# Moving the second conv chunk's taps, the staging slots and the first banks of the down product in a decoder layer's kernel

## The chip, the core and the metric

The kernel runs on one core of one Trainium2 chip. The metric is the device time of one execution in microseconds; several executions are timed and their median is given. One further execution is recorded by the hardware profiler, and all rows of a trace come from that one.

## What is computed

One layer of a hybrid decoder on 1024 tokens and 16 meta tokens put in front of them (T = 1040 rows of 1024 channels), all in float32:

```
h = LN(concat(meta, x))
z = h @ w_in + b_in   ->  q | k | v | c_val, c_gate | g_attn, g_conv
a = attention(q, k, v)          # window 128, 8 heads, 2 key heads, a sink each, 16 meta keys for all
c = silu(LN(dwconv31(c_val * sigmoid(c_gate))))
mixed = sigmoid(g_attn) * (a @ w_attn_proj) + sigmoid(g_conv) * (c @ w_conv_proj)
h = LN(alpha * h + mixed @ w_out)
u, g = dwconv3(h @ ffn_w_up)
out = LN(alpha * h + (gelu(g) * u) @ ffn_w_down)   # the 16 meta rows are dropped
```

The depthwise convolution over 31 taps has 512 channels: four chunks of 128 channels, one per partition.

## The kernel before

**Order of the work.** The program is written once, in a sequence, and a scheduler then fixes the order on each engine and each DMA queue when the kernel is built. It plays the program through with its own cost of every instruction; of those that are due by then, the one with the lowest number in `cur_priority` (or in a `rank` around it) goes next. `after(a, b)` puts a behind b in that order and adds no wait. On the chip each engine runs its own list strictly in that order, and SP's list holds most DMA issues, so an instruction that waits holds up everything behind it in its list. Waits come from data alone: a write waits for earlier readers and writers of the same columns of a tile. The tile FA (128 x 6144 float32) is used by many steps one after the other, and its column ranges count, not its names.

**Precision.** TensorE multiplies in a reduced float32 form, so every operand is split in two: a high half by a ScalarE copy and a low half by a VectorE subtraction (L303 to L307 for weights). Each product takes three matmuls (`product`, L338): lines 342, 345 and 346.

**The z stage (L349 on).** The product h @ w_in is made in tiles of 128 output channels; each takes 8 x 3 matmuls for each of four column groups (`z_group`). There are three PSUM banks for the groups (`ps_z`, tag "mm", bufs=3), and each is emptied by its own `evac`. The first three tiles (k, v, q of the first head pair) are written out by hand in three groups of 272, 384 and 384 columns (L482 to L646). The residual products (L293, L294), 18 of them on VectorE, keep the normalized input times alpha for later.

**Staging slots.** `stage(n)` (L368) gives a place in FA where ScalarE puts an evicted group before it goes on: k on its way to DRAM (L377), q before its split (L393, L395, L396), a gate's sigmoid (L695, L696), a merge gate's tanh (L724). Before, there are five slots, 400 columns apart, from column 4104.

**Conv chunks (L689).** A chunk makes its gate tile (`g_evac`, tanh by ScalarE), then its value tile, whose groups VectorE multiplies with the sigmoid into `cin` (`v_evac2`, L703). `cin` has two buffers, taken in turn: chunk 1, chunk 0, chunk 2, chunk 3. Then 31 taps follow on VectorE, one instruction each over 1026 columns (L713 the first, L715 the other thirty), into `acc[c]`, at a rank behind everything else (60000 and 100 more for each chunk). The coefficients `cdw` are loaded at L671. Chunks 1 and 0 come before attention; chunks 2 and 3 come between the merge gates (`order`, L930), which are the work that fills TensorE while attention waits.

**Values and keys.** `vT` = FA[:, 0:1040] holds v transposed. It is turned back by transposes on TensorE (L766, L774) and split (L769, L778, L779). k comes back from DRAM into FA from column 2054 (`kr`, L748) and is copied to `Kx` (L755, L757). `vd` is a broadcast of the bias table to all partitions in DRAM, from which the bias tiles are read (L730 on).

**Attention.** For each block and each head one bank `ps_s` is filled (L887, L888) and emptied by VectorE (L891), and then come exponentials, transposes (L911) and the product with v (L922 to L924).

**Up and down products.** The up product (L1526) uses four tiles of two PSUM banks each, in this order: pw, px, pz, py. The last one to be written in each pass is py, and VectorE empties it (L1534). The result f goes to DRAM (`f_out`, L1462). The down product has eight accumulators of one bank each: `X` and `Z`, four each (L1583). Its operands come in pairs (f and weights) from `operand` (L1603): a load into a raw place, then the two split instructions (L1613, L1614). Six pairs are made ahead.

```
F_RAW = [RXF[:, 0:1024], RXF[:, 1024:2048]] + [FA[:, i * 1024:(i + 1) * 1024] for i in range(6)]
W_RAW = [None, None] + [OB[:, i * 1024:(i + 1) * 1024] for i in (2, 3, 0, 1)]
```

`None` is one of two weight buffers. Columns 0 to 4096 of FA also hold the temporaries of the up product's convolution (`ftmp`), eight of 512 columns in turn.

Of the kernel before, what the change touches and what calls it, by code (L numbers as in the profile page):

```python
# [29 lines left out]
P = 128  # L30
# [82 lines left out]
def tile_hybrid_layer(  # L113
# [6 lines left out]
    def dram(ap, offset, dims):  # L120
        return bass.AP(tensor=ap.tensor, offset=ap.offset + offset, ap=[list(d) for d in dims])

    def load(o, i):
        return nc.sync.dma_start(out=o, in_=i)
# [156 lines left out]
    def h0(k, hl, a, b):  # L281
        return (RHO, RHC)[hl][:, k * T + a:k * T + b]
# [34 lines left out]
        return [t[:, o:o + D] for o in W_FLAT]  # L317

    fills, cin_done, gate_mm, gate_last = [0], [], {}, []
    last_fill, last_split = [], []  # L320

    def weights(shape, fill):
        fills[0] += 1
# [14 lines left out]
    def product(ps, terms, behind=None):  # L338

        n = len(terms)  # L340
        for i, (ah, al, bh, bl) in enumerate(terms):
            ins = nc.tensor.matmul(ps, al, bh, start=i == 0, stop=False)  # L342
            if i == 0 and behind is not None:
                after(ins, behind)
            nc.tensor.matmul(ps, ah, bh, start=False, stop=False)  # L345
            last = nc.tensor.matmul(ps, ah, bl, start=False, stop=i == n - 1)  # L346
        return last

    def z_group(wt, g, a, b, evac):  # L349
        hi, lo = wt  # L350
        ps = pat.tile([P, 512], F, name="ps_z", tag="mm", bufs=3)
        last = product(ps[:, :b - a], [(hi[:, k], lo[:, k], h0(k, 0, a, b), h0(k, 1, a, b)) for k in range(KC)])
        with rank(RK_EVAC):
            evac(g, a, b, ps[:, :b - a])
        return last
# [9 lines left out]

    st_next = [0]

    def stage(n, lo=4104, cnt=5):  # L368
        i = st_next[0] % cnt
        st_next[0] += 1  # L370
        return FA[:, lo + i * 400:lo + i * 400 + n]

    tc.cur_priority = RK_QKV + 1000

# [293 lines left out]
    att = ExitStack()  # L668
    cp = att.enter_context(tc.tile_pool(name="cin", bufs=2, side="right", reuse_waits="tile"))
    cdw = cp.tile([P, TAPS * CH], F, name="cdw", tag="cdw", bufs=1)  # L670
    load(cdw, cols_in[:, n_kept:])  # L671
    ap = att.enter_context(tc.tile_pool(name="att", bufs=1, side="right", reuse_waits="tile"))

    Kx = [ap.tile([P, NB, 144], R, name=f"kx{g}") for g in range(NKV)]
# [9 lines left out]
    tc.cur_priority = RK_QKV + 1000  # L684


    acc = [FA[:, c * U:(c + 1) * U] for c in range(CH)]

    def conv_chunk(c):  # L689
        sig = {}  # L690
# [36 lines left out]
        gate_mm[i] = z_tile(in_cols(14 + i), TG, gate_evac)  # L727

    tc.cur_priority = RK_QKV + 2000
    after(load(vd, dram(v1d, 0, [[0, P], [J_LEN, NH], [1, J_LEN]])), last_fill[-1])  # L730
    load(bias[:, :, 0:P], dram(vd, 127, [[L8 - 1, P], [J_LEN, NH], [1, P]]))
    load(bias[:, :, 144:272], dram(vd, 127 + P, [[L8 - 1, P], [J_LEN, NH], [1, P]]))
    load(bias[:, :, P:144], dram(vd, J_META, [[L8, P], [J_LEN, NH], [1, 16]]))
# [1 line left out]
    load(biasq, dram(vd, J_METAQ + 1, [[L8 - 1, 2], [J_LEN, NH], [1, 16]]))  # L735

    tc.cur_priority = RK_QKV + 4000
    taps = [conv_chunk(1)]
    cin4 = cin_done[-1]
    vmT = ap.tile([P, 64], F, name="vmT")  # L740
    after(nc.vector.memset(vmT, 0.0), cin4)
    for hl in range(2):
        for g in range(NKV):
            vm_ins = nc.vector.tensor_copy(vmT[g * HD:(g + 1) * HD, hl * 32 + g * 16:hl * 32 + g * 16 + 16],
                                  vT[g * HD:(g + 1) * HD, 0:16])
    tc.cur_priority = RK_QKV + 1000
    for g in range(NKV):
        kr = FA[:, 2054 + g * T:2054 + (g + 1) * T]  # L748
        for h in range(2):
            load(kr[h * HD:(h + 1) * HD, :T], kd[g * HD:(g + 1) * HD, :])  # L750
        for lo in (0, 64):
            for o, i in ((Kx[g][lo:, :, 16:144], kr[lo:, 16:T].rearrange("p (n c) -> p n c", c=P)),
                         (Kx[g][lo:, :, 0:16], kr[lo:, 0:16].unsqueeze(1).to_broadcast([P - lo, NB, 16]))):
                if lo == 0:
                    ins = nc.vector.tensor_copy(o, i)  # L755
                else:
                    ins = nc.vector.tensor_tensor(o, i, f32(o), OP.subtract)  # L757
                after(ins, vm_ins)
    ones = ones_of(cp, vm_ins)
    for t in [vm] + pmTs:  # L760
        after(nc.vector.memset(f32(t[64:]), 0.0), vm_ins)
    tc.cur_priority = RK_QKV + 4000
    taps.append(conv_chunk(0))
    tc.cur_priority = RK_QKV + 2000
    ps = pat.tile([P, 512], F, name="ps_vm", tag="t", bufs=2)
    after(nc.tensor.transpose(ps[:64, :P], vmT, ident), gate_last[-1][2])  # L766
    src = ps[:64, :P].rearrange("p (g d) -> p g d", d=HD)
    nc.scalar.copy(vm[:64, :, 0], src)
    nc.vector.tensor_tensor(vm[:64, :, 1], src, f32(vm[:64, :, 0]), OP.subtract)  # L769
    for q4 in range(2):  # L770
        ps = pat.tile([P, 512], F, name="ps_v4", tag="t", bufs=2)
        for i in range(4):
            c = NMETA + (q4 * 4 + i) * P
            after(nc.tensor.transpose(ps[:, i * P:(i + 1) * P], vT[:, c:c + P], ident), gate_last[-1][2])  # L774
        src = ps[:, :].rearrange("p (n g d) -> p n g d", g=2, d=HD)
        for g in range(NKV):
            hi, lo = (V[:, q4 * 4:q4 * 4 + 4, g, i] for i in range(2))
            nc.scalar.copy(hi, src[:, :, g, :])  # L778
            nc.vector.tensor_tensor(lo, src[:, :, g, :], f32(hi), OP.subtract)  # L779
    for t in taps:  # L780
        t()
    tc.cur_priority = RK_QKV + 5000
    for r in range(1, 4):
        z_tile(in_cols(r), TG, q_evac(r))


# [793 lines left out]
    oa_stack.close()  # L1580
    dn = ctx.enter_context(tc.tile_pool(name="dn", bufs=1, side="left", reuse_waits="tile"))
    pdn = ctx.enter_context(tc.tile_pool(name="pdn", bufs=1, space=PSUM, reuse_waits="tile"))
    X, Z = ([pdn.tile([P, 512], F, name=f"ps_{n}", tag=f"d{j}") for j in b]  # L1583
            for n, b in (("x", (0, 1, 6, 7)), ("z", (2, 3, 4, 5))))


    def blk(t, first, step, col):
# [8 lines left out]
    W_DN = [(OC, OC_UP + i * 2048) for i in range(4)] + [(RHC, 4096 + R_DN), (RHC, 6144 + R_DN), (RHO, 6144 + R_DN)]  # L1596
    F_RAW = [RXF[:, 0:1024], RXF[:, 1024:2048]] + [FA[:, i * 1024:(i + 1) * 1024] for i in range(6)]
    W_RAW = [None, None] + [OB[:, i * 1024:(i + 1) * 1024] for i in (2, 3, 0, 1)]
    PAIRS = [(j, min(2, FH - j)) for j in range(0, FH, 2)]

    los, evacs = [], []

    def operand(i, src, j, n, raws, places):  # L1603
        raw = raws[i % len(raws)]
        if raw is None:
            raw = wraw([P, D])
        raw = raw[:, :n * 512]
# [5 lines left out]
        nc.scalar.copy(hi, raw)  # L1613
        los.append(nc.vector.tensor_tensor(lo, raw, f32(hi), OP.subtract))  # L1614
        if len(los) > 1:
            after(los[-1], evacs.pop() if evacs else los[-2])
        return hi, lo
# [187 lines left out]
```

## Time and profile before

| | |
|---|---|
| three timed executions | 1282.48, 1283.21, 1283.51 us; median 1283.21 |
| the profiled execution | 1284.34 us, span 1282.6 us from first to last instruction |
| mean granted clock of TensorE | 0.992 |
| instructions | 23049 |
| DMA | 212.19 MB, 165 GB/s on average |

How to read the rows: times are microseconds from the start of the span. A row of the timeline has start, duration, engine (PE = TensorE, PEld its weight loads, DVE = VectorE, ACT = ScalarE, SPq and ACTq the DMA issues of SyncE and ScalarE), line, operation, what is written <- what is read, shapes, count, and in brackets the engine's idle time before it and what ended that. In the slices of the page, each digit is a fortieth of the span, in tenths. A row of waits has the total, the number of times and the longest. A row of a stretch has its length, the busy time of PE, PEld, DVE, ACT and POOL with counts, the granted clock, the DMA share and GB/s.

### The profile page before, as it was taken

Reading aid. Unit: us, or ns where it says so; the run is one execution under the profiler, and the core shown is the slowest. Engines: PE = TensorE matmul, PEld = TensorE weight load, DVE = VectorE, ACT = ScalarE, POOL = GpSimd, SP = SyncE. Lnnn points to the kernel's source line nnn. Section 1 sums busy time; section 2 is a strip of 40 time slices with the busy share of each in tenths; the row PEclk is TensorE's granted clock in tenths of the full one; section 3 lists DMA queues with packets and bytes.
Section 4 is the critical chain, followed back from the end, with each engine's and each line's share of the span. In section 5 each row is a group of like instructions: output and inputs, shape, how many; then the busy total and the mean of one; then the engine's idle time right before and its main releaser. Section 6 shows DMA issues by size and latency. Waiting matters only on the chain.

```text
span 1282.6 us, 23049 instructions
## 1 busy us (share of the span) xinstructions
PE 1260.1 (98%) x9194; PEld 1187.8 (93%) x9194; DVE 1076.1 (84%) x1862; ACT 586.0 (46%) x1080; POOL 18.6 (1%) x16
## 2 busy tenths in 40 slices
PE   7999998999999999999999999999999999999997
PEld 7899998999999999788899999999999997888886
DVE  7879999999969466547899999999899986888697
ACT  5423344555455232344654554555555553535330
POOL 2200000001000000000000000000000000000000
PEclk8999998999999999999999999999999999999999
DMA  6275742432445565222235455453455556989722
GB/s 247 82 243 144 185 116 73 120 89 76 111 117 146 158 170 141 91 83 83 83 105 206 174 208 177 186 211 123 164 189 191 193 204 240 394 289 389 264 75 82
DMA packets 98701, 212.19 MB, mean 165 GB/s; under 512 B 11411, under 2 KB 38611, under 8 KB 98338
## 3 DMA queue, kind: packets, MB, share of 16 engines
q1 hardware_dynamic: 84474, 199.64, 46.7%
q10 hardware_dynamic: 14120, 11.08, 2.8%
q8 instruction: 72, 1.18, 0.4%
q14 instruction: 35, 0.29, 0.1%
HBM read 150.29 MB, written 62.70 MB: 166 GB/s over the span
## 4 chain that ended last, share of the span: by engine, by line
PE 92%; DVE 5%; DMA 1%; issue 1%; ACT 1%; SPq 0%; POOL 0%; DVEq 0%; ACTq 0%
PE px L1526 14%; PE py L1526 9%; PE ps_x L1651 9%; PE ps_z L342 8%; PE ps_z L346 8%; PE ps_z L345 8%; PE ps_z L1651 5%; PE pz L1526 5%; PE pw L1526 5%; PE ps_p L346 2%; PE ps_p L342 2%; PE ps_p L345 2%; PE ps_w L346 2%; PE ps_w L342 2%; PE ps_w L345 2%; PE ps_z L548 1%
## 5 line engine op out<-in xcount | busy, mean ns | idle before, releaser
L346 PE MATMUL ps_z<-RHC,w 128*128 128x256 f32 (+2 forms) x864 | 244.5, 283 | 0.0
L342 PE MATMUL ps_z<-RHO,w 128*128 128x256 f32 (+2 forms) x864 | 244.5, 283 | 0.0
L345 PE MATMUL ps_z<-RHO,w 128*128 128x256 f32 (+2 forms) x864 | 243.8, 282 | 0.0
L342 PEld LDWEIGHTS ps_z<-RHO,w 128*128 128x128 f32 x864 | 163.2, 189 | 0.9 <-issue 0.3
L346 PEld LDWEIGHTS ps_z<-RHC,w 128*128 128x128 f32 x864 | 163.4, 189 | 0.6
L345 PEld LDWEIGHTS ps_z<-RHO,w 128*128 128x128 f32 x864 | 163.3, 189 | 0.4
L715 DVE SCALAR_TENSOR_TENSOR FA<-cin,cdw,FA 128x1026 f32<-128x1026 f32 x120 | 152.3, 1278 | 0.2
L1348 DVE TENSOR_TENSOR RHO<-wr,RHO 128x512 fp32r<-128x512 f32 x94 | 63.8, 687 | 7.9 <-ACT RHO L1347 7.8
L1347 ACT CAST RHO<-wr 128x512 fp32r<-128x512 f32 x94 | 56.7, 619 | 25.7 <-DVE wr L1365 11.6
L307 DVE TENSOR_TENSOR w<-wr,w 128x1024 fp32r<-128x1024 f32 x37 | 45.1, 1219 | 26.8 <-ACT w L304 26.7
L304 ACT CAST w<-wr 128x1024 fp32r<-128x1024 f32 x37 | 38.8, 1047 | 54.7 <-PE ps_z L346 36.4
L1365 DVE TENSOR_TENSOR wr<-wr 128x512 f32<-128x512 f32 x88 | 60.4, 686 | 0.1
L724 ACT ACTIVATE FA<-ps_z,colr 128x258 f32<-128x258 f32 (+1 forms) x64 | 30.1, 471 | 58.9 <-PE ps_z L346 48.3
L1538 ACT COPY FA<-px 128x514 f32<-128x514 f32 (+2 forms) x23 | 13.1, 571 | 76.5 <-PE px L1526 76.5
L1348 DVE TENSOR_TENSOR w<-wr,w 128x512 fp32r<-128x512 f32 x60 | 40.7, 688 | 4.9 <-ACT w L1347 4.7
L1526 PE MATMUL px<-OA,RHO 128*128 128x258 f32 x324 | 43.2, 282 | 0.0
L1453 ACT ACTIVATE FA<-OB,coll 128x512 f32<-128x512 f32 x44 | 35.9, 815 | 14.6 <-DVE OB L1534 14.6
L1347 ACT CAST w<-wr 128x512 fp32r<-128x512 f32 x60 | 36.3, 618 | 12.8 <-DVE wr L1365 6.4
L1526 PE MATMUL px<-RHC,RHO 128*128 128x258 f32 (+1 forms) x312 | 41.1, 281 | 0.8 <-ACT OB L1538 0.8
L1526 PE MATMUL px<-OC,RHO 128*128 128x256 f32 x324 | 41.5, 277 | 0.0
L1538 ACT COPY OB<-px 128x514 f32<-128x514 f32 (+2 forms) x46 | 26.1, 567 | 32.1 <-PE px L1526 31.9
L1526 PEld LDWEIGHTS px<-OA,RHO 128*128 128x128 f32 x324 | 40.5, 189 | 0.2 <-ACT OB L1538 0.2
(441 smaller groups left out, 3314.2 us busy)
## 6 DMA issues: line engine op xcount, KB each, us to landing
wr<-in_w_up_dram SPq DMA_DIRECT2D x44, 512.0 KB, 3.6
wr<-in_w_z_dram SPq DMA_DIRECT2D x29, 512.0 KB, 3.9
fd<-FA SPq DMA_DIRECT2D x44, 256.0 KB, 2.1
OB<-in_w_down_dram SPq DMA_DIRECT2D x21, 512.0 KB, 3.7
FA<-sd SPq DMA_DIRECT2D x15, 512.0 KB, 9.1
qt<-qd SPq DMA_DIRECT2D x28, 256.0 KB, 4.1
sgd<-FA ACTq DMA_DIRECT2D x48, 128.0 KB, 2.4
td<-OB SPq DMA_DIRECT2D x12, 512.0 KB, 2.6
```

The source lines that it names most:

```text
L304: ins = nc.scalar.copy(hi, raw)
L307: return nc.vector.tensor_tensor(lo, raw, f32(hi), OP.subtract)
L342: ins = nc.tensor.matmul(ps, al, bh, start=i == 0, stop=False)
L345: nc.tensor.matmul(ps, ah, bh, start=False, stop=False)
L346: last = nc.tensor.matmul(ps, ah, bl, start=False, stop=i == n - 1)
L715: nc.vector.scalar_tensor_tensor(acc[c], cin[:, j:j + U], wc, acc[c], OP.mult, OP.add)
L1347: nc.scalar.copy(hi, src)
L1348: ins = nc.vector.tensor_tensor(lo, src, f32(hi), OP.subtract)
L1365: ins = nc.vector.tensor_tensor(*x)
L1526: ins = nc.tensor.matmul(o, x[:, ks], bmat(sub, q, hl, k), start=first and k + j == 0, stop=k == 3 and j == 2, skip_group_check=not first)
L1538: copied.append(nc.scalar.copy(*x))
L1651: nc.tensor.matmul(banks[i], l[:, ts], r[:, ws], start=first and a and x + k == 0, stop=z and x == len(ops) - 1 and k == 2, skip_group_che ...
```

## The change

It has seven parts.

1. `z_group` puts the first matmul of each group behind the last of the group before it in the program, for all groups that it makes.
2. `stage` has seven slots, 280 columns apart, from column 4146, in place of five, 400 apart, from 4104.
3. `acc` lies at columns 0, 1040, 2066 and 3092 in place of 0, 1026, 2052 and 3078, so that acc[1] no longer shares columns with `vT`; `kr` moves to 2066 and ends where the slots begin.
4. The load of `vd` is put behind the load of `cdw`.
5. Chunk 1's taps are called right behind its input; chunk 0's taps stay behind the V transposes. K copies, memsets and the meta values come behind chunk 0's input rather than chunk 1's.
6. q tile 1 comes ahead of the V transposes, which were behind the third group of chunk 0's gate.
7. The down product's accumulators are allocated in the order of their numbers; X is 0, 1, 6, 7 as before and Z is 4, 5, 2, 3. The first six operand pairs use raw places 0, 1, 2, 3, 0, 1, and the later ones go on from place 4.

```diff
-        last = product(ps[:, :b - a], [(hi[:, k], lo[:, k], h0(k, 0, a, b), h0(k, 1, a, b)) for k in range(KC)])
+        last = product(ps[:, :b - a], [(hi[:, k], lo[:, k], h0(k, 0, a, b), h0(k, 1, a, b)) for k in range(KC)],
+                       z_last[-1] if z_last else None)
+        z_last.append(last)
...
-    def stage(n, lo=4104, cnt=5):
+    def stage(n, lo=3 * T + U, cnt=7):
         i = st_next[0] % cnt
         st_next[0] += 1
-        return FA[:, lo + i * 400:lo + i * 400 + n]
+        return FA[:, lo + i * 280:lo + i * 280 + n]
...
-    load(cdw, cols_in[:, n_kept:])
+    cdw_in = load(cdw, cols_in[:, n_kept:])
...
-    acc = [FA[:, c * U:(c + 1) * U] for c in range(CH)]
+    acc = [FA[:, a:a + U] for a in (0, T, T + U, T + 2 * U)]
...
-    after(load(vd, dram(v1d, 0, [[0, P], [J_LEN, NH], [1, J_LEN]])), last_fill[-1])
+    ins = load(vd, dram(v1d, 0, [[0, P], [J_LEN, NH], [1, J_LEN]]))
+    after(ins, last_fill[-1])
+    after(ins, cdw_in)
...
-    taps = [conv_chunk(1)]
-    cin4 = cin_done[-1]
+    conv_chunk(1)()
+    taps = conv_chunk(0)
+    tc.cur_priority = RK_QKV + 5000
+    cin8 = cin_done[-1]
+    ones = ones_of(cp, cin8)
     vmT = ap.tile([P, 64], F, name="vmT")
-    after(nc.vector.memset(vmT, 0.0), cin4)
...
+    for t in (f32(vm[64:]), f32(pmTs[0][64:]), f32(pmTs[1][64:]), vmT):
+        after(nc.vector.memset(t, 0.0), cin8)
     for g in range(NKV):
-        kr = FA[:, 2054 + g * T:2054 + (g + 1) * T]
+        kr = FA[:, T + U + g * T:T + U + (g + 1) * T]
...
-                after(ins, vm_ins)
-    ones = ones_of(cp, vm_ins)
...
-    taps.append(conv_chunk(0))
-    tc.cur_priority = RK_QKV + 2000
+                after(ins, cin8)
...
+    q1 = z_tile(in_cols(1), TG, q_evac(1))
     ps = pat.tile([P, 512], F, name="ps_vm", tag="t", bufs=2)
-    after(nc.tensor.transpose(ps[:64, :P], vmT, ident), gate_last[-1][2])
+    after(nc.tensor.transpose(ps[:64, :P], vmT, ident), q1[-1])
...
-            after(nc.tensor.transpose(ps[:, i * P:(i + 1) * P], vT[:, c:c + P], ident), gate_last[-1][2])
+            after(nc.tensor.transpose(ps[:, i * P:(i + 1) * P], vT[:, c:c + P], ident), q1[-1])
...
-    for t in taps:
-        t()
-    tc.cur_priority = RK_QKV + 5000
-    for r in range(1, 4):
+    taps()
+    for r in range(2, 4):
         z_tile(in_cols(r), TG, q_evac(r))
...
-    X, Z = ([pdn.tile([P, 512], F, name=f"ps_{n}", tag=f"d{j}") for j in b]
-            for n, b in (("x", (0, 1, 6, 7)), ("z", (2, 3, 4, 5))))
+    D8 = [pdn.tile([P, 512], F, name="ps_" + "xxzzzzxx"[j], tag=f"d{j}") for j in range(8)]
+    X, Z = ([D8[j] for j in b] for b in ((0, 1, 6, 7), (4, 5, 2, 3)))
...
+    def place(i, n):
+
+        return i % 4 if i < 6 else (i - 2) % n
...
-        raw = raws[i % len(raws)]
+        raw = raws[place(i, len(raws))]
```

More of the change, by code (lines that the diff above doesn't have):

```diff
@@ L319, in tile_hybrid_layer @@
     fills, cin_done, gate_mm, gate_last = [0], [], {}, []
-    last_fill, last_split = [], []
+    last_fill, last_split, z_last = [], [], []
     def weights(shape, fill):
@@ L737, in tile_hybrid_layer @@
     tc.cur_priority = RK_QKV + 4000
-    taps = [conv_chunk(1)]
-    cin4 = cin_done[-1]
-    vmT = ap.tile([P, 64], F, name="vmT")
-    after(nc.vector.memset(vmT, 0.0), cin4)
[L742 to L746, printed above, removed]
+    conv_chunk(1)()
[3 more added lines that the diff above has]
+    ones = ones_of(cp, cin8)
+    vmT = ap.tile([P, 64], F, name="vmT")
+    for t in (f32(vm[64:]), f32(pmTs[0][64:]), f32(pmTs[1][64:]), vmT):
+        after(nc.vector.memset(t, 0.0), cin8)
     for g in range(NKV):
-        kr = FA[:, 2054 + g * T:2054 + (g + 1) * T]
+        kr = FA[:, T + U + g * T:T + U + (g + 1) * T]
         for h in range(2):
@@ L757, in tile_hybrid_layer @@
                     ins = nc.vector.tensor_tensor(o, i, f32(o), OP.subtract)
-                after(ins, vm_ins)
-    ones = ones_of(cp, vm_ins)
-    for t in [vm] + pmTs:
-        after(nc.vector.memset(f32(t[64:]), 0.0), vm_ins)
-    tc.cur_priority = RK_QKV + 4000
-    taps.append(conv_chunk(0))
-    tc.cur_priority = RK_QKV + 2000
+                after(ins, cin8)
+    for hl in range(2):
+        for g in range(NKV):
+            nc.vector.tensor_copy(vmT[g * HD:(g + 1) * HD, hl * 32 + g * 16:hl * 32 + g * 16 + 16],
+                                  vT[g * HD:(g + 1) * HD, 0:16])
+    q1 = z_tile(in_cols(1), TG, q_evac(1))
     ps = pat.tile([P, 512], F, name="ps_vm", tag="t", bufs=2)
-    after(nc.tensor.transpose(ps[:64, :P], vmT, ident), gate_last[-1][2])
+    after(nc.tensor.transpose(ps[:64, :P], vmT, ident), q1[-1])
     src = ps[:64, :P].rearrange("p (g d) -> p g d", d=HD)
```

## The prediction

> **What bounds the kernel now.** The page of the profile comes first: busy time, then the slices.
>
> ```profile
> PE 1260.1 (98%) x9194; PEld 1187.8 (93%) x9194; DVE 1076.1 (84%) x1862; ACT 586.0 (46%) x1080; POOL 18.6 (1%) x16
> ...
> PE   7999998999999999999999999999999999999997
> ...
> PEclk8999998999999999999999999999999999999999
> ```
>
> TensorE is busy for 1260.1 of 1282.6 us, so only 22.5 us are idle, and no change of order can win more than those and what a slow clock costs. The seventh slice (192 to 224 us) is the one place inside the run where both PE and its clock fall below 9. The waits of PE tell who ends the idle time, and three stretches tell what it costs (in each: length, PE busy, PEld, DVE, ACT, POOL, then granted clock).
>
> ```profile
> PE ps_s L887 <- DVE sm L891: 2.8, 2, 2.3
> ...
> PE pw L1526 <- ACT FA L1328: 1.0, 1, 1.0
> PE ps_z L1651 <- ACT RHC L1613: 1.0, 1, 1.0
> ...
> PE px L1526 <- ACT OB L1538: 0.8, 1, 0.8
> PE ps_z L1651 <- DVE OB L1534: 0.7, 1, 0.7
> ...
> 192.00:198.27 6.27, 3.32 (x25) 2.68 (x24) 6.24 (x14) 2.29 (x8) 0.00 (x0) 1.00 0.03 8
> 198.27:205.10 6.83, 6.17 (x27) 5.60 (x28) 6.67 (x20) 1.14 (x4) 0.00 (x0) 0.50 0.30 75
> ...
> 1062.20:1072.00 9.80, 9.09 (x41) 7.21 (x41) 9.80 (x13) 6.04 (x7) 0.00 (x0) 1.00 0.50 190
> ```
>
> PE idles 2.95 us from 192.00 to 198.27 and 0.66 us after it, 3.6 together. Then 6.17 busy microseconds run at half clock: 6.17 / 2 = 3.1 us more. So this hole costs **6.7 us**. The joint to the down product, with 0.7 and 1.0, costs 1.7. The rest lies in the first 65 us and at the end, where the change moves little.
>
> **Why there is a hole at 193 us.** The timeline of PE and of DVE:
>
> ```profile
> 191.83 0.28 PE L346 MATMUL ps_z<-RHC,w 128*128 128x256 f32 x1
> ...
> 202.01 0.41 PE L342 MATMUL ps_z<-RHO,w 128*128 128x256 f32 x1
> ...
> 201.16 1.28 DVE L703 SCALAR_TENSOR_TENSOR cin<-ps_z,colr,FA 128x272 f32<-128x272 f32 x3
> ...
> 201.10:211.90 10.80, 5.13 (x4) 0.82 0.21 50
> ```
>
> From 191.83 to 202.01 PE has no z matmul to fill attention's waits. These are chunk 2's value groups: three fill all three ps_z banks, and DVE evicts them only at 201.16. They go to the first of two cin buffers, which chunk 1 holds until its 31st tap. The last row (taps alone, 201.10 to 211.90) shows four taps still to come: they are chunk 0's. So the two chunks' taps alternate, and chunk 1, begun a few taps ahead, ends just before.
>
> **The change, part by part.**
>
> *Taps, values, coefficients.*
>
> ```profile
> 87.93 0.29 PE L345 MATMUL ps_z<-RHO,w 128*128 128x272 f32 x1
> ...
> 94.49 0.48 DVE L703 SCALAR_TENSOR_TENSOR cin<-ps_z,colr,FA 128x256 f32<-128x256 f32 x1 [4.51 <-PE ps_z L346]
> ...
> 105.80 0.82 DVE L713 TENSOR_SCALAR FA<-cin,cdw,colr 128x1026 f32<-128x1026 f32 x1 [0.24 <-PE ps_v L774]
> ...
> 115.78 0.81 DVE L713 TENSOR_SCALAR FA<-cin,cdw,colr 128x1026 f32<-128x1026 f32 x1
> ...
> 90.40 0.58 SPq L124 DMA_DIRECT2D cdw<-in_cols_dram  x1
> ...
> SPq L124 <- DMA vd<-v1d: 10.6, 1, 10.6
> ...
> 95.00:157.00 62.00, 62.00 (x533) 62.00 (x533) 58.94 (x78) 22.06 (x44) 0.00 (x0) 1.00 0.66 171
> ...
> 105.80:131.00 25.20, 18.39 (x15) 1.00 0.54 144
> 131.00:175.60 44.60, 32.76 (x27) 1.00 0.58 153
> ```
>
> Chunk 1's first tap runs at 105.80, released by the V transposes (L774): acc[1] began 14 columns inside vT. Chunk 0's runs at 115.78. The new places remove that overlap for chunk 1 alone; acc[0] still lies on vT, and its taps now wait for transposes behind q tile 1, four z groups later. Those are 96 matmuls, and 533 took 62.00 us here, so 11.2 us: about 126 to 131. The group order ends chunk 1's value tile before chunk 0's gate starts: two gate groups (the first is 272 wide, from 87.93) no longer run inside its last group, and its last cin (94.49) comes 48 matmuls, 5.6 us, sooner. The coefficients, issued just behind the vd broadcast on whose landing SP then waits 10.6 us, go ahead of it and should land by about 93 instead of somewhere up to 101.
>
> So chunk 1 has the taps to itself until about 131. The K copies and memsets move behind chunk 0's input but cost DVE the same. Before, 2 + 15 taps were done by 131 for both chunks; now about 17, all of chunk 1's. It needs 14 more, or 28 alternating ones; before, 27 took 131.0 to 175.6. Its buffer is free near 177, while the value groups that need it start at about 182. **The hole closes with some ten microseconds to spare**: 6.7 us. A DVE lagging by that much would still not reopen it. What would be late next is attention's own chain, and between 206 us and the joint PE waits only twice by the list above, for pw and px of the up product. Bounds: 3.6 (the half clock stays) to 6.7.
>
> *The staging slots.* Here I expect a new wait. There are seven slots 280 columns apart, but the first k and q groups are 384 wide, so they run into the next slot. Counting calls: k and q of group 0 take slots 0 and 1, then q 2, k 3, k 4, q 5, and chunk 1's first gate group takes slot 6, whose first 104 columns lie under q's slot 5. Before, it had a slot long free.
>
> ```profile
> 52.99 0.34 ACTq L128 DMA_DIRECT2D kd<-FA  x1
> ...
> 57.15 0.57 ACT L377 ACTIVATE FA<-ps_z,colr 128x384 f32<-128x384 f32 x1
> 57.76 0.33 ACTq L128 DMA_DIRECT2D kd<-FA  x1
> ...
> 64.66 0.58 ACT L393 ACTIVATE FA<-ps_z,qb 128x384 f32<-128x384 f32 x1 [2.70 <-PE ps_z L548]
> ...
> 67.70 0.49 ACT L695 ACTIVATE FA<-ps_z,colr 128x272 f32<-128x272 f32 x1 [0.20 <-PE ps_z L346]
> ...
> 102.87 0.49 ACT L695 ACTIVATE FA<-ps_z,colr 128x272 f32<-128x272 f32 x1
> ...
> 73.04 0.28 PE L342 MATMUL ps_z<-RHO,w 128*128 128x256 f32 x1
> ...
> 76.36 0.54 DVE L396 TENSOR_TENSOR qsl<-FA,qsh 128x384 fp32r<-128x384 f32 x1
> 76.83 6.05 DVE L294 SCALAR_TENSOR_TENSOR x<-x,r,gb 128x1024 f32<-128x1024 f32 x5
> ...
> 100.27 2.77 DVE L757 TENSOR_TENSOR kx<-FA,kx 64x1024 fp32r<-64x1024 f32 x4
> ```
>
> The reader of that q slot is the low half's subtraction (L396). DVE reaches it only at 76.36, eleven microseconds after q's third group was evicted (64.66 + 0.58), because residual products (L293, L294) lie in front of it in DVE's fixed order. The tanh at 67.70 must then wait until 76.9. Such overlaps bind: before, chunk 0's first gate group was held in just this way by the K copies (102.87 against 100.27 + 2.77), sharing 30 columns with kr. Behind the tanh on ACT are the other gate evictions and a weight split. PE fills its three banks up to 73.04 and needs the first one back: 76.9 + 0.5 for the tanh = 77.4. **New idle: 77.4 - 73.0 = 4.4 us.** Nothing gives it back, since PE is the bound for the next hundred microseconds. The two other new overlaps fall on finished work: k's third group (57.15) on a store issued at 52.99, q's (64.66) on one of 57.76. Bounds of this wait: 0 (DVE reaches the subtraction early) and 10.9 (it comes behind the five further products, at 83.4; a tanh more is 83.9).
>
> *V transposes behind q1, group order after 120 us, kr and vd loads:* the same instructions in other places, beside a busy PE, with V and K first wanted at 157 or later; 0, between -0.5 and +0.5 (the 0.48 of one eviction on DVE by which a bank may come sooner or later).
>
> *The joint.*
>
> ```profile
> 1065.86 0.73 PE L1651 MATMUL ps_z<-OC,RHC 128*128 128x512 f32 x2 [0.71 <-DVE OB L1534]
> ...
> 1086.17 2.00 PE L1651 MATMUL ps_z<-RHC,RHO 128*128 128x512 f32 x6 [0.97 <-ACT RHC L1613]
> ...
> 1079.59 0.37 SPq L124 DMA_DIRECT2D FA<-fd  x1
> ...
> 1084.42 1.22 DVE L1614 TENSOR_TENSOR RHO<-FA,RHO 128x1024 fp32r<-128x1024 f32 x1 [6.90 <-ACT RHO L1613]
> ```
>
> Z's third bank is py, which the last up product writes and DVE evicts; in the new numbering Z takes pz and px, free earlier: 0.7 gone. The second wait is the fifth operand pair, whose load must follow the last f store, since it reuses its columns; from RXF and the weight buffers it can be loaded before that store instead of at 1079.59: 1.0 gone. Its splits (two of 1.22 on DVE) then come ahead of the last f chain and may delay its store by 2.4, and the sixth and seventh pairs with it; I take 1.7, between 0.7 (the bank alone) and 2.6 (half as much again for PE's restart after each wait).
>
> **Sum.** -6.7 + 4.4 - 1.7 = **-4.0 us**. The profiled execution took 1284.34 (span 1282.6 and 1.7 around it), 1.1 over the median of three runs, 1283.21; from the median, 1279.2.
>
> **The rivals.**
> 1. *Half clock after the new wait.* A stretch with 3.32 of 6.27 us busy was followed by one at 0.50, the joint's with 9.09 of 9.80 by none. The new 4.4 us leave 2.4 of 6.8 busy if they fall in one such stretch, and about 4.6 in each if they straddle two. It costs 6.83 / 2 = 3.4: 1282.6. The Trainium skill, "TensorE: Matmul & The Clock Gate", section "HAM oscillation — how this bites in real kernels", allows no idle gap above about 3.4 us, which speaks for this rival and against the change. The trace agrees only in part: a longest wait of 2.3 us, with more beside it, was enough here.
> 2. *No new wait,* if DVE gets to the subtraction near 66 us. For it: its rank is higher than the residual's. Against: it had that rank before and ran at 76.36. -6.7 - 1.7: 1274.8.
> 3. *Slower.* The subtraction slides behind the five further products. PE waits 10.9, surely with half clock: -8.4 + 10.9 + 3.4 = +5.9, 1289.1. It decides from the point where the subtraction ends after 81 us (4.0 later than now), or after 77.5 with half clock.
> 4. *The change doesn't do what it says:* chunk 0, whose taps rank ahead, takes DVE from 131 on; chunk 1 needs 31 + 14 = 45 more taps, where 42 took until 201. The hole stays: -1.7 + 4.4, 1285.9. The alternation seen above speaks against it.
>
> **Chances.** Forecast 0.42, half clock 0.22, no wait 0.20, slower 0.10, hole stays 0.06. 0.2% is 2.6 us, about what a measurement of this kernel can tell from no change. Faster by more (below 1280.6): no wait, most of the forecast and a little of the half clock, 0.58; slower (above 1285.8): 0.14; between: 0.28. The range 1274.4 to 1284.2 takes in the first three cases with the joint's bounds and leaves out rivals 3 and 4.
>
> **What would show it.** PE from 73 to 77.5: a wait of ps_z for ACT, and the first chunk-1 tanh (L695 before) ending behind the subtraction from qsl. Around 193: no wait on L891, clock 1.00, chunk 2's first cin written before the third bank is needed. First tap near 93 and two first taps over 30 us apart. At the joint no wait on py and none on the fifth pair. The forecast is wrong if the hole's place fills but PE idles elsewhere between 90 and 210, which would mean that the fixed order moved a wait that this trace doesn't show.

## The result, and the profile after

The kernel after takes 1277.47 us (median of five executions, 1275.49 to 1277.78), the kernel before beside it 1283.21 (five, 1282.48 to 1284.24). The ratio is 0.9951, with a 95% interval of 0.9937 to 0.9966: 4.4 to 8.1 us faster. The two profiled executions took 1284.34 and 1277.78, with spans of 1282.6 and 1276.0.

The page of the profile after, busy time and slices:

```profile
PE 1255.9 (98%) x9194; PEld 1185.9 (93%) x9194; DVE 1078.4 (85%) x1862; ACT 587.0 (46%) x1080; POOL 19.5 (2%) x16
...
PE   7999999999999999999999999999999999999997
...
PEclk8999999999999999999999999999999999999999
```

The seventh slice is 9 in both rows now. The waits of PE after, those of over 0.4 us behind the first 65:

```profile
PE ps_x L1655 <- ACT RHO L1617: 1.0, 1, 1.0
PE pw L1526 <- ACT FA L1328: 1.0, 1, 1.0
PE ps_x L1655 <- DVE RHO L1618: 0.5, 1, 0.5
```

The wait for L891 is gone. There is no wait for a z bank near 73 us, which was forecast, and at the joint two new ones stand in place of the two old. Three starts divide the span: the first z matmul made by `z_group`, the first one of the product behind attention (`ps_p`), the first of the down product. Before:

```profile
64.46 0.29 PE L342 MATMUL ps_z<-RHO,w 128*128 128x272 f32 x1
...
433.77 0.28 PE L342 MATMUL ps_p<-OA,w 128*128 128x258 f32 x1
...
1062.24 0.40 PE L1651 MATMUL ps_z<-OC,RHC 128*128 128x512 f32 x1
```

After:

```profile
65.32 0.29 PE L342 MATMUL ps_z<-RHO,w 128*128 128x272 f32 x1
...
427.62 0.28 PE L342 MATMUL ps_p<-OA,w 128*128 128x258 f32 x1
...
1056.22 0.40 PE L1655 MATMUL ps_z<-OC,RHC 128*128 128x512 f32 x1
```

| stage | before | after | difference |
|---|---|---|---|
| up to the first z group | 64.46 | 65.32 | +0.9 |
| from there to `ps_p`, with the hole and the staging slots | 369.31 | 362.30 | **-7.0** |
| to the down product | 628.47 | 628.60 | +0.1 |
| down product and end | 220.4 | 219.8 | -0.6 |
| span | 1282.6 | 1276.0 | -6.6 |

I do not count the first row to the change: in the profiles of the experiments that start comes between 62.99 and 64.48, 62.99 in a kernel that differs from this one only in SP's list near the end. The second row is the whole gain that the profiles show. It repeats well: the three experiments below that change the kernel after only at the down product take 362.28, 362.30 and 362.31 there, and the one that changes the kernel before only there takes 369.60. The last row does not repeat: the profiles of the six experiments below whose kernels have the down product exactly as after have 219.7 to 223.2 there, so the -0.6 shows nothing. Two stretches around the old hole, after (length, PE busy, PEld, DVE, ACT, POOL, granted clock):

```profile
186.00:196.00 10.00, 10.00 (x88) 10.00 (x87) 9.94 (x26) 4.07 (x14) 0.00 (x0) 1.00 0.39 106
196.00:206.00 10.00, 10.00 (x84) 9.87 (x84) 9.65 (x22) 5.47 (x15) 0.00 (x0) 1.00 0.32 75
```

And VectorE's timeline after, the four moments that decide it:

```profile
91.53 0.82 DVE L715 TENSOR_SCALAR FA<-cin,cdw,colr 128x1026 f32<-128x1026 f32 x1 [0.48 <-DMA cdw<-in_cols_dram]
...
131.19 0.81 DVE L715 TENSOR_SCALAR FA<-cin,cdw,colr 128x1026 f32<-128x1026 f32 x1
...
172.76 0.07 DVE L702 MEMSET cin<- 128x16 f32 x1
...
188.31 0.48 DVE L705 SCALAR_TENSOR_TENSOR cin<-ps_z,colr,FA 128x272 f32<-128x272 f32 x1
```

Chunk 1's first tap, chunk 0's first tap, chunk 1's buffer taken over by chunk 2 (its 31st tap is done), and chunk 2's first input: the buffer is free 15.5 us before the input comes. (Lines of the conv chunk, of attention's splits and of the down product stand two to five higher than before.)

### The profile page after: what moved, and what is told of

Its sections match the earlier page's. It is cut to its first block, busy times and chain, and to the rows that moved or that the text cites. A ratio compares the mean times of both kernels' runs of the same rounds, so it can differ in the third digit from the quotient of the medians.

```text
span 1276.0 us, 23038 instructions
## 1 busy us (share of the span) xinstructions
PE 1255.9 (98%) x9194; PEld 1185.9 (93%) x9194; DVE 1078.4 (85%) x1862; ACT 587.0 (46%) x1080; POOL 19.5 (2%) x16
## 4 chain that ended last, share of the span: by engine, by line
PE 88%; DVE 6%; DMA 2%; ACT 1%; issue 1%; SPq 1%; POOL 0%; DVEq 0%; ACTq 0%
PE px L1526 14%; PE py L1526 9%; PE ps_x L1655 9%; PE ps_z L342 8%; PE ps_z L346 7%; PE ps_z L345 7%; PE ps_z L1655 5%; PE pw L1526 5%; PE pz L1526 4%; PE ps_p L346 2%; PE ps_p L342 2%; PE ps_p L345 2%; PE ps_w L346 2%; PE ps_w L342 2%; PE ps_w L345 2%; PE ps_t L911 1%
## 5 line engine op out<-in xcount | busy, mean ns | idle before, releaser
L1538 ACT COPY OB<-px 128x514 f32<-128x514 f32 (+2 forms) x46 | 26.1, 566 | 31.8 <-PE px L1526 31.6
```

What stands on the lines that cost most here:

```text
L1538: copied.append(nc.scalar.copy(*x))
```

## The experiments

Two counts are used below. "To `ps_p`" is the second row of the table above, which leaves the start out. The **head start** is the number of chunk 1's taps that VectorE has done when chunk 0's first one comes; after that the two chunks take turns, so chunk 1's buffer comes free after about h + 2(31 - h) = 62 - h of all taps.

### Was it the buffer?

```diff
-        cin = cp.tile([P, 16 + T], F, name="cin", tag="cin")
+        cin = cp.tile([P, 16 + T], F, name="cin", tag="cin" if c in (1, 3) else "cin2", bufs=1)
```

> The kernel after, but chunk 2's input takes the buffer of chunk 0 instead of that of chunk 1 (the two inputs get a buffer by name, one each); places, order of calls and loads stay as after. Theory A (the hole at 193 us is the wait of chunk 2's value groups for a buffer that a chunk's taps still hold): chunk 0's taps run until about 203 or later, as they did before, so the hole comes back at about 190 to 205 us with chunk 2's first input beside it, and costs 5 to 8 us: about 1284, 1281 to 1288. Rival B (the hole went because the value groups, the K copies or the loads stand at other places in the fixed order): no change, 1277.5 within 1.

Measured: 1289.76 us, ratio to before 1.0048 (1.0030 to 1.0065), 12.4 us over the kernel after by the ratios; 374.84 to `ps_p` against 362.30. One of the stretches, and chunk 2's first inputs:

```profile
201.00:208.00 7.00, 5.14 (x21) 3.97 (x22) 6.88 (x22) 3.77 (x12) 0.00 (x0) 0.75 0.32 79
```

```profile
215.38 1.27 DVE L705 SCALAR_TENSOR_TENSOR cin<-ps_z,colr,FA 128x272 f32<-128x272 f32 x3
```

Places, loads and calls are those of the kernel after, and so is the head start (19); only the buffer is another (chunk 3's input and a later sum of two chunks change buffers with it). The hole is back with the slow clock of before; it begins some four microseconds later, near 196, and lasts longer. So the buffer is the cause. It is larger than I expected, since chunk 0's buffer comes free after all 62 taps, at 215 and not at 203.

```diff
-    acc = [FA[:, a:a + U] for a in (0, T, T + U, T + 2 * U)]
+    acc = [FA[:, a:a + U] for a in (0, U, T + U, T + 2 * U)]
...
-    conv_chunk(1)()
-    taps = conv_chunk(0)
+    taps = [conv_chunk(1), conv_chunk(0)]
...
-    taps()
+    for t in taps:
+        t()
```

> The kernel after, but chunk 1's accumulator begins again 14 columns inside vT, and both chunks' taps are called behind the V transposes. These stand behind q tile 1, so chunk 1's first tap cannot come before about 126 to 131 us. Theory A (the hole is the wait for chunk 1's buffer, freed by its 31st tap): 15 to 17 taps that ran before 131 us are lost, some 20 us of VectorE's time beside attention, so the hole comes back larger than in the kernel before: 10 to 35 us, about 1297. Rival B (the order of groups and loads closed the hole): 1277.5 within 1.

Measured: 1307.17 us, ratio 1.0186 (1.0172 to 1.0199); 394.06 to `ps_p`, 31.8 more than after. Both first taps run together, and chunk 2's input waits for nearly all of both chunks:

```profile
127.58 1.54 DVE L715 TENSOR_SCALAR FA<-cin,cdw,colr 128x1026 f32<-128x1026 f32 x2 [0.83 <-PE ps_v L775]
...
238.97 1.28 DVE L705 SCALAR_TENSOR_TENSOR cin<-ps_z,colr,FA 128x272 f32<-128x272 f32 x3
```

Head start 0: the worst case of the count. The edit changes the columns and the place of the calls together; that the first tap's wait ends with a V transpose (L775) points to the 14 shared columns, but no run has the one change without the other.

### Which parts made the head start?

The columns alone, on the kernel before:

```diff
-    def stage(n, lo=4104, cnt=5):
+    def stage(n, lo=4118, cnt=5):
...
-    acc = [FA[:, c * U:(c + 1) * U] for c in range(CH)]
+    acc = [FA[:, a:a + U] for a in (0, T, T + U, T + 2 * U)]
...
-        kr = FA[:, 2054 + g * T:2054 + (g + 1) * T]
+        kr = FA[:, T + U + g * T:T + U + (g + 1) * T]
```

> The kernel before, with the columns alone changed: acc at 0, 1040, 2066 and 3092, kr at 2066 and the five staging slots from 4118 (400 apart as before); order of calls, loads and groups as before. Theory (each part removes some of the delay of chunk 1's first tap): with the columns apart the V transposes no longer hold it, and it waits for the coefficients instead, which still stand behind the load of vd: first tap at about 103 in place of 105.80. Chunk 0's taps still start near 116, so the two chunks still share VectorE, and the hole shrinks only in part: 1 to 3 us won, 1280 to 1282. Rival: the columns alone are the whole gain, 6.7 us: 1276.5. Second rival: chunk 1's buffer is free no sooner, 1283.2.

Measured: 1291.86 us, ratio 1.0063 (1.0049 to 1.0076): **8 us slower than before**. All three expectations were wrong. VectorE's timeline, then PE's:

```profile
100.85 0.82 DVE L713 TENSOR_SCALAR FA<-cin,cdw,colr 128x1026 f32<-128x1026 f32 x1 [6.13 <-DMA cdw<-in_cols_dram]
101.58 0.71 DVE L744 COPY vmT<-FA 64x16 f32<-64x16 f32 x4
```

```profile
102.43 0.39 PE L766 MATMUL ps_vm<-coll,vmT 128*64 128x128 f32 x1 [4.22 <-DVE vmT L744]
```

Freed of the shared columns, the first tap was put at the head of VectorE's fixed order, where the scheduler thought its coefficients there. They were not: VectorE stood still for 6.13 us with the vmT copies queued behind, and the transposes that wait for those copies held PE for 4.22. With a second wait of 2.0 behind it and the clock at 0.83 from 96 to 116 us, that is 6.2 + 20 x 0.17 = 9.6 us lost; the hole later shrank by some 2. The same without part 4, on the kernel after:

```diff
-    after(ins, cdw_in)
```

> The kernel after, without part 4: the coefficients are loaded behind the vd broadcast again, everything else as after. What the run with the columns alone showed (a first tap that stands ready in VectorE's list but waits 6.1 us for its coefficients holds all that follows it) should show here too: first tap at about 101 us instead of 91.5, behind it seven more taps and then the weight split and the input of chunk 0, which TensorE needs at about 103: TensorE idles 5 to 9 us between 100 and 115, 1283 to 1287. Rival A (the coefficients only start the taps sooner, and the hole has some ten microseconds to spare): 1277.5 within 0.5. Rival B (the lost ten microseconds bring the hole at 193 us back): waits at 190 to 205, about 1284 too, but with them in that place.

Measured: 1284.98 us, ratio 1.0013 (1.0003 to 1.0023), the whole gain gone. VectorE's timeline, PE's wait, and two stretches:

```profile
100.70 0.82 DVE L715 TENSOR_SCALAR FA<-cin,cdw,colr 128x1026 f32<-128x1026 f32 x1 [9.28 <-DMA cdw<-in_cols_dram]
101.56 9.24 DVE L717 SCALAR_TENSOR_TENSOR FA<-cin,cdw,FA 128x1026 f32<-128x1026 f32 x7
110.71 1.22 DVE L307 TENSOR_TENSOR w<-wr,w 128x1024 fp32r<-128x1024 f32 x1
...
113.05 0.49 DVE L705 SCALAR_TENSOR_TENSOR cin<-ps_z,colr,FA 128x272 f32<-128x272 f32 x1
```

```profile
PE ps_z L342 <- DVE cin L705: 5.6, 1, 5.6
```

```profile
106.00:116.00 10.00, 4.41 (x29) 4.21 (x28) 9.89 (x10) 0.00 (x0) 0.00 (x0) 0.71 0.39 96
...
196.00:206.00 10.00, 10.00 (x89) 10.00 (x88) 9.84 (x27) 4.50 (x17) 0.00 (x0) 1.00 0.26 72
```

The first tap is 9.2 us later, and the split and input of chunk 0 queued behind it are late for PE. But at 196 to 206 PE is full: the hole did not come back (rival B fell). This is no test of the spare time at the buffer, since the wait held TensorE up too: chunk 2 takes the buffer 8.3 us later than after, and its first input comes 6.9 us later, so 14.2 us are left between the two.

```profile
181.05 0.07 DVE L702 MEMSET cin<- 128x16 f32 x1
...
195.21 0.48 DVE L705 SCALAR_TENSOR_TENSOR cin<-ps_z,colr,FA 128x272 f32<-128x272 f32 x1
```

Part 4's worth is not at the hole; it pays because VectorE's order has the tap ahead of work that PE needs.

Then columns and part 4 together on the kernel before:

```diff
-    load(cdw, cols_in[:, n_kept:])
+    cdw_in = load(cdw, cols_in[:, n_kept:])
...
+    after(ins, cdw_in)
```

> The kernel before, with the columns of the run before (parts 2 and 3, five slots) and part 4, the coefficients ahead of vd. VectorE's list is the one that lost 9.4 us before attention. Theory: that loss was the wait for the coefficients at the head of this list; it goes, the first tap runs at about 95, and of the hole at 193 us 2 to 6.7 us go: 1276.5 to 1281.5, likeliest 1279. Rival (the loss came from the tap's place ahead of the V and K copies, not from its wait): still slower than before, 1286 to 1291.

Measured: 1283.03 us, ratio 0.9998 (0.9989 to 1.0007). The loss of the columns is gone, so it was the wait for the coefficients. But the gain is not there, and the forecast of 1279 was wrong: a wait of 1.5 us at 102 us is new, and of the hole about half is left. The stretch there, and chunk 0's first tap:

```profile
196.00:206.00 10.00, 8.52 (x57) 8.10 (x57) 9.84 (x28) 4.25 (x14) 0.00 (x0) 0.83 0.23 54
```

```profile
115.44 0.80 DVE L713 TENSOR_SCALAR FA<-cin,cdw,colr 128x1026 f32<-128x1026 f32 x1
```

Chunk 1 starts at 94.38 instead of 105.80, but chunk 0 still starts at 115.44, and between them VectorE does the K copies, memsets and V values: seven taps of head start against six, 56 taps until the buffer is free against 57. Part 6 added to this:

```diff
+    q1 = z_tile(in_cols(1), TG, q_evac(1))
     ps = pat.tile([P, 512], F, name="ps_vm", tag="t", bufs=2)
-    after(nc.tensor.transpose(ps[:64, :P], vmT, ident), gate_last[-1][2])
+    after(nc.tensor.transpose(ps[:64, :P], vmT, ident), q1[-1])
...
-            after(nc.tensor.transpose(ps[:, i * P:(i + 1) * P], vT[:, c:c + P], ident), gate_last[-1][2])
+            after(nc.tensor.transpose(ps[:, i * P:(i + 1) * P], vT[:, c:c + P], ident), q1[-1])
```

> The kernel of the run before this one with columns and coefficients, and part 6 beside them: q tile 1 ahead of the V transposes. Theory (what counts is how many taps chunk 1 has done when chunk 0's first one comes: 6 in the kernel before and 7 with columns and coefficients, so that chunk 1's buffer came free after 56 of all taps; 19 in the kernel after, and 45): here chunk 0's taps are held by vT until the transposes behind q tile 1, chunk 1 gets about 17 taps ahead, its buffer is free after about 46 and the hole goes: 1277.5 to 1279.5, the wait of 1.5 us near 104 us may stay. Rival (the K copies and memsets on VectorE between 95 and 108 us, part 5's second half, are what delays chunk 1): the hole stays, 1283.

Measured: 1280.81 us, ratio 0.9975 (0.9964 to 0.9986). VectorE's and PE's timelines, and the stretch of the hole:

```profile
132.42 0.80 DVE L713 TENSOR_SCALAR FA<-cin,cdw,colr 128x1026 f32<-128x1026 f32 x1
```

```profile
102.26 0.36 PE L342 MATMUL ps_z<-RHO,w 128*128 128x272 f32 x1 [2.08 <-ACT FA L696]
```

```profile
196.00:206.00 10.00, 10.00 (x89) 10.00 (x88) 9.85 (x24) 5.89 (x17) 0.00 (x0) 1.00 0.41 106
```

Chunk 0's first tap moves to 132.42, held by vT; the head start is 17, chunk 2's buffer is free after 46 taps, and the hole is gone with the K copies where they were before. To `ps_p` it takes 364.79, 3.0 less than without part 6 and 2.5 more than after; the 2.08 us wait at 102 is most of that rest. The median is above the range that I gave. In this profile that wait and the down product account for it (222.7 us against 220.4 in the kernel before, whose down product this kernel has); but the profiled execution, 1282.43 us, is itself 1.6 over the median.

| kernel | head start | all taps done when chunk 2 takes the buffer | to `ps_p` | ratio to before |
|---|---|---|---|---|
| before | 6 | 57 | 369.31 | 1 |
| columns | 7 | 56 | 376.70 | 1.0063 |
| columns, part 4 | 7 | 56 | 367.80 | 0.9998 |
| columns, parts 4 and 6 | 17 | 46 | 364.79 | 0.9975 |
| after without part 4 | 19 | 44 | 370.91 | 1.0013 |
| after | 19 | 44 | 362.30 | 0.9951 |

In every row the count is 62 - h and one more. The head start alone does not give the time: the columns and the kernel after without part 4 lose time at waits before 115 us, not only at the buffer.

### The wait that was forecast at 73 us

The trace after shows the tanh (L697) late, as forecast, and PE not waiting. ScalarE, then VectorE, then the stretch:

```profile
71.34 0.47 ACT L697 ACTIVATE FA<-ps_z,colr 128x256 f32<-128x256 f32 x1 [2.98 <-PE ps_z L346]
...
74.10 0.47 ACT L697 ACTIVATE FA<-ps_z,colr 128x256 f32<-128x256 f32 x1 [1.74 <-PE ps_z L346]
...
79.72 0.47 ACT L697 ACTIVATE FA<-ps_z,colr 128x272 f32<-128x272 f32 x1
```

```profile
77.23 0.54 DVE L398 TENSOR_TENSOR qsl<-FA,qsh 128x384 fp32r<-128x384 f32 x1
```

```profile
73.00:81.00 8.00, 8.00 (x62) 6.92 (x60) 8.00 (x8) 3.82 (x7) 0.00 (x0) 1.00 0.78 290
```

The first group (the only one of 272 columns) is evicted last of the four, behind the subtraction; the other three, from 71.34 on, pass it. PE is busy throughout, so the groups behind must have used the two banks that the second and the third group gave back. So the overlap binds and costs nothing. Two kernels test that. First, the four tanhs pinned in order:

```diff
-            nc.scalar.activation(sig[g], ps, AF.Tanh, bias=bcol(10 + c), scale=0.5)
+            ins = nc.scalar.activation(sig[g], ps, AF.Tanh, bias=bcol(10 + c), scale=0.5)
+            if c == 1 and g:
+                after(ins, tanhs[-1])
+            tanhs.append(ins)
```

> The kernel after, but the four tanhs of chunk 1's gate are pinned in the order of their groups on ScalarE, so that the first one, which waits for the low half of q's third group, has the other three behind it. Theory: the wait that the prediction put at 73 us is real where the other evictions cannot pass: the tanh ends at 77.7 to 79.7, the fourth group finds no free bank, TensorE idles 4 to 7 us from about 73: 1281.9, up to 1285 with half clock behind it. Rival: TensorE does not depend on these banks there (other groups have the banks, or the subtraction comes sooner): 1277.5 within 1, and no wait of ps_z for ACT near 75 us.

Measured: 1284.94 us, ratio 1.0006 (0.9997 to 1.0015), 7.1 us over the kernel after by the ratios; 368.30 to `ps_p`, 6.0 more. PE's timeline and two stretches of this kernel:

```profile
78.10 0.58 PE L342 MATMUL ps_z<-RHO,w 128*128 128x256 f32 x1 [4.57 <-ACT FA L699]
```

```profile
73.00:81.00 8.00, 3.43 (x16) 3.00 (x15) 8.00 (x9) 3.70 (x7) 0.00 (x0) 0.81 0.98 368
...
1090.00:1100.00 10.00, 7.23 (x24) 5.15 (x23) 5.50 (x5) 4.29 (x5) 0.00 (x0) 0.83 1.04 393
```

With the first tanh in front, PE waits 4.57 us, which is the 4.4 of the prediction, and the clock behind it falls (0.81): the wait and 8.00 x 0.19 = 1.5 of clock make the 6. Second, slots that do not overlap:

```diff
-    def stage(n, lo=3 * T + U, cnt=7):
+    def stage(n, lo=3 * T + U, cnt=5):
...
-        return FA[:, lo + i * 280:lo + i * 280 + n]
+        return FA[:, lo + i * 399:lo + i * 399 + n]
```

> The kernel after, with five staging slots 399 columns apart from column 4146, so that no slot runs into the next. Theory: the overlap of the slots held chunk 1's first gate tanh to about 79.7 us but cost TensorE nothing, so the tanh comes back to about 68.5 and the time stays: 1277.5 within 0.5. Rival: the tanh's delay, or the missing two slots, moves the stages behind it: 1 to 3 us either way (1274.5 to 1280.5), seen in TensorE's waits before 105 us.

Measured: 1278.23 us, ratio 0.9961 (0.9948 to 0.9974). ScalarE's timeline:

```profile
67.33 0.49 ACT L697 ACTIVATE FA<-ps_z,colr 128x272 f32<-128x272 f32 x1 [0.20 <-PE ps_z L346]
```

The tanh comes 12.4 us sooner and nothing is won: 362.07 to `ps_p` against 362.30. Neither the overlap nor the number of slots matters by itself here.

### The joint

Part 7 taken back, and part 7 alone on the kernel before:

```diff
-    D8 = [pdn.tile([P, 512], F, name="ps_" + "xxzzzzxx"[j], tag=f"d{j}") for j in range(8)]
-    X, Z = ([D8[j] for j in b] for b in ((0, 1, 6, 7), (4, 5, 2, 3)))
+    X, Z = ([pdn.tile([P, 512], F, name=f"ps_{n}", tag=f"d{j}") for j in b]
+            for n, b in (("x", (0, 1, 6, 7)), ("z", (2, 3, 4, 5))))
...
-        raw = raws[place(i, len(raws))]
+        raw = raws[i % len(raws)]
```

> The kernel after, with the down product's accumulators and the raw places of its operands as they were before (part 7 taken back alone). By the trace after, part 7 removed two waits (0.7 and 1.0) but made the seventh operand pair late (1.0 and 0.5), and from the first down matmul to the last it won 0.6 us: without it 1278.1. By the prediction's term: 1.7 us, 1279.2. If part 7 is worth nothing: 1277.5.

> The kernel before, with part 7 (banks and raw places of the down product) added alone. By the trace after 0.6 us: 1282.6 where the kernel before takes 1283.2, with waits of ps_x for the seventh pair in place of those on py and on the fifth pair. By the prediction's term 1.7 us: 1281.5. If part 7's value comes only with the rest: 1283.2.

Measured: 1276.49 us without it (ratio 0.9942, 0.9928 to 0.9956) and 1284.00 with it alone (1.0001, 0.9992 to 1.0009). As it stands part 7 is worth nothing that can be measured; both medians lean the other way, within their intervals. The down product and the end take 220.4 us without and 219.8 with it after, 220.1 with it alone; by the spread named under the stage table these differences show nothing. SP's list after shows what holds the seventh pair:

```profile
1076.66 1.75 SPq L124 DMA_DIRECT2D w<-fd  x2
1078.47 0.43 SPq L124 DMA_DIRECT2D FA<-fd  x1
1078.99 0.51 SPq L124 DMA_DIRECT2D OB<-in_w_down_dram  x1
```

The 1 MB load of the sums is issued ahead of the seventh pair's two loads. One step later in that list:

```diff
-    steps([(sums_load, FC - 2)], [(gain_rows, 0)], [(sums_last, FC - 2), (row, 4, 0)], [(row, 5, 0)], [(row, 6, 0)],
+    steps([], [(sums_load, FC - 2), (gain_rows, 0)], [(sums_last, FC - 2), (row, 4, 0)], [(row, 5, 0)], [(row, 6, 0)],
```

> The kernel after, but the 1 MB load of the sums is called one step later in the up product's last part, so that the loads of the seventh operand pair of the down product stand ahead of it in SP's list. Theory: the two waits of ps_x for the seventh pair's splits (1.0 and 0.5) come from its loads standing behind that load: both go, 1276.0, 1275.5 to 1276.7. Rival 1: the pair is late because its place in FA becomes free only with the last f store, and the waits stay: 1277.5. Rival 2: what needs the sums becomes late and the waits move there: 1277.5 to 1280.

Measured: 1275.28 us, ratio 0.9933 (0.9921 to 0.9946), the lowest median of the study. The issues, and all that is left of PE's waits at the joint:

```profile
1073.99 0.42 SPq L124 DMA_DIRECT2D FA<-fd  x1
1074.53 1.26 SPq L124 DMA_DIRECT2D OB<-in_w_down_dram  x1
1075.88 0.91 SPq L124 DMA_DIRECT2D w<-fd  x2
```

```profile
PE ps_x L1655 <- ACT OC L1617: 0.4, 1, 0.4
```

The two waits for the seventh pair are gone, so it was the load of the sums that held it. Down product and end take 218.7 us, 1.1 less than after and 1.0 less than the shortest of the six with the down product of the kernel after. The medians differ by more, but the intervals overlap; a gain in time is not shown. Last, the same place of the sums without part 7:

> The kernel after, without part 7 and with the load of the sums one step later. Theory: part 7 wins its 1.7 us only where the seventh pair's loads do not stand behind the load of the sums; here the waits of the kernel before on py and on the fifth pair (0.6 and 1.1) stay, the seventh pair was not late without part 7, and the sums' place changes nothing: 1276.5 to 1277.5, and 211.9 to 212.4 us from the first matmul of the down product to the last, against 210.7 with part 7 and the later sums. Rival: the later sums alone bring the gain: 210.7 and 1275.3.

Measured: 1276.18 us, ratio 0.9943 (0.9931 to 0.9955); 1053.77 to 1266.12, so 212.35 from the first matmul of the down product to its last, against 210.70 with part 7. Its waits are the old ones:

```profile
PE ps_z L1655 <- ACT RHC L1617: 1.1, 1, 1.1
PE ps_z L1655 <- DVE OB L1534: 0.6, 1, 0.6
```

By these profiles the sums' place alone brings nothing, and with part 7 the two bring 1.65 us, near the 1.7 of the prediction. That rests on one profile of each kernel. The seven kernels with the down product of the kernel after, itself among them, take 211.7 to 215.2 us from first to last; their first wait for the seventh pair is between 1.0 and 2.2 us, and in three of them the clock drops to 0.83 beside it. What makes that wait longer or shorter stays open.

## Why the prediction was right, and where it was wrong

The forecast was 1279.2 us, with a range of 1274.4 to 1284.2; the time is 1277.47. From the profiles it said -4.0 and got -6.6 (-5.7 by the medians): two steps were off, in opposite directions. Without the 4.4 us of new wait the same sum gives 1274.8. That the time lies nearer to 1279.2 is in part luck: the joint's gain of 1.7 did not show, and the start was 0.9 later for reasons outside the change. The lower end of the range does not quite hold what it was said to hold: rival 2 with the joint's bound of 2.6 is 1273.9.

- **The hole, 6.7 us: right, by its own mechanism.** 7.0 went. Chunk 0's first tap was forecast at 126 to 131 and came at 131.2; about 17 taps were to be done by then and 19 were; chunk 1's buffer was to be free near 177 and was at 172.8. The experiment with the swapped buffer shows the cause. The spare time was forecast at some ten microseconds and is 15.5 in the trace after; no run takes it away. What the prediction did not see is that the parts are not separate terms: by themselves the columns lose 8 us, columns with coefficients win nothing, and without the coefficients the kernel after has no gain left.
- **The staging slots, +4.4 us: the step that failed.** "PE fills its three banks up to 73.04 and needs the first one back": it needs one back, and not the first. The tanh was late, as worked out (79.7 against 76.9), but in ScalarE's order the other three evictions pass the held one, and the next groups went on in the two banks that these gave back. The prediction had put them behind it ("Behind the tanh on ACT are the other gate evictions"). With that order pinned, PE waits 4.57 us: the size was right, the order was not. The row for it stood in the prediction: chunk 0's first gate group was held in just that way until 102.87 in the kernel before, and PE had no wait there.
- **No new wait (rival 2)** came true in its effect, but not by its reason: VectorE did the subtraction at 77.23, as late as forecast. Rival 1's condition (clock after a long wait) held where the wait was forced: 0.81, but it cost 1.5 us there and not 3.4.
- **V transposes and order of the groups, 0:** in the run that adds part 6 it is worth 3.0 us, because it holds chunk 0's taps back. The prediction had used this effect, but in the hole's term, so the 0 is not a miss of the sum; as the price of the part it is wrong.
- **The joint, -1.7 us: mis-sized, 0.6 in the trace,** which is within the spread of one profile to the next, and nothing in the medians. The two old waits went, as forecast, and two of 1.0 and 0.5 for the seventh pair came. No run shows a price for "PE's restart after each wait", which made the upper bound. The clause that the seventh pair may come later was the right one; what holds it is the sums' load in SP's list, not the f store that was named.

Open: which of the later moves (the K copies, or the slots' start behind kr) removes the wait near 102 us that is left with columns and parts 4 and 6. In that run the held gate group waits 2.57 us for a K copy, with which its slot shares columns; in the kernel after the copies come later and the slots lie elsewhere, and no run separates the two. The pinned order of the groups (part 1) was not run by itself either.

## What to carry to other kernels

Before you price a held eviction, look in the issuing engine's order for what stands behind it: where the others could pass, it cost nothing here, and where it stood first, 4.57 us of waiting were paid. An instruction that is released from one wait moves up in an order fixed at build time, and its next wait, for a load that the scheduler thought landed, is then paid by everything queued behind it: release the operands together or not at all. Where two streams take turns on one engine, each step of head start brings the first one's end one step forward, so delaying the second can be the gain.

## What the runs showed of the hardware that was not expected

The clock fell behind waits that were each short. At the joint of the kernel with the pinned tanhs, waits of 2.2 and 0.5 us left 7.23 us busy out of 10, and the granted clock of that stretch was 0.83; after, waits of 1.0 and 0.5 cost no clock:

```profile
1086.00:1096.00 10.00, 8.49 (x37) 6.45 (x36) 7.80 (x9) 5.26 (x6) 0.00 (x0) 1.00 1.04 390
```

The Trainium skill, "TensorE: Matmul & The Clock Gate", section "HAM oscillation — how this bites in real kernels", puts the limit at an idle gap of about 3.4 us. The 4.57 us wait of the pinned tanhs, with 0.81 in its stretch, agrees; the joint above, with a longest wait of 2.2, does not.

The sizes of the waits do not settle it either. At the joint with columns and parts 4 and 6, waits of 1.43 and 0.53 us had the slow clock beside them; with the swapped buffer, 1.64 and 0.76 had not. The two stretches, the swapped buffer first:

```profile
1092.00:1102.00 10.00, 7.61 (x33) 5.74 (x32) 3.15 (x3) 2.72 (x3) 0.00 (x0) 1.00 1.02 385
```

```profile
1078.00:1088.00 10.00, 8.04 (x28) 5.85 (x27) 4.06 (x5) 4.42 (x6) 0.00 (x0) 0.83 1.03 392
```

What decides it stays open.
